# Neighbourhood scores of a hybrid attention block: a low part on 64 rows, or on both halves of 128

## The chip, the core and the metric

The kernel runs on one core of a Trainium2 chip. The metric is the device time of one execution in microseconds (us); less is better. Three runs are shown and their median is taken. The profile is of one execution more. Engine names are those of the profile: PE is TensorE's matmul side, PEld its weight loads, DVE is VectorE, ACT is ScalarE, POOL is GpSimd, and SP issues the DMAs.

## What is computed

Two layers of a block for 256 image tokens (a 4 x 64 grid) and 256 context tokens, 1024 wide, in float32. In each layer both streams are normed and modulated, projected, sent through three branches (neighbourhood attention, a gated MLP, a low-rank attention called MLA), merged by gates, projected out, and sent through a squared-ReLU MLP. In the second layer only the image stream is finished. The part that matters here is the neighbourhood attention with 8 heads of 64 dims:

```python
q_na = rms_norm(split_heads(cols(p, OFF_NA_Q, NA_WIDTH), NA_HEADS), na_q_gain[i])
k_na = rms_norm(split_heads(cols(p, OFF_NA_K, NA_WIDTH), NA_HEADS), na_k_gain[i])
...
s_loc = jnp.einsum('bhqd,bhkcd->bhqkc', q_r, k_band).astype(jnp.float32) * scale + bias
s_loc = jnp.where(col_in[:, None, :], s_loc, NEG_INF).reshape(b, h, GRID_W, kh * GRID_W)
s_ctx = jnp.einsum('bhqd,bhld->bhql', q_r, k_ctx).astype(jnp.float32) * scale
p = jax.nn.softmax(jnp.concatenate([s_loc, s_ctx], axis=-1), axis=-1).astype(v.dtype)
```

In the first layer the context's queries attend to the context's keys too, without the bias.

## The kernel before

**Products in two parts.** Most products take float32 operands as a sum of two float32r tiles, a high part H and a low part L (`split1`, L115 and L116: ACT writes `wh`, DVE subtracts to get `wl`). A product of two such operands is three matmuls: H by H, H by L, L by H (`mm3`, L276 to L278). These carry nearly all of PE's time: the projections (`b_ps`, `u`), the gates and branch products (`gate`, `z`), the output (`o_ps`) and the MLP (`f`).

**Scores.** Heads have 64 dims, and the array has 128 rows, so the score product is packed. `na_keys` (L352) puts a head's H part on the head's own half of the partitions (rows 0 to 63 for even heads, 64 to 127 for odd ones) and its L part on the other half, in one tile `naK`. `na_queries` (L367) transposes two heads at a time into PSUM (`tr_ps`), lets ACT write the query's H part on both halves of a tile `naQ` (L377, L378), and lets DVE write the L part on the head's own half of a tile `naQL` that two heads share (L379). `na_score` (L384) then needs two matmuls for a score block: `naQ` by `naK` over 128 rows (L389: H by H and H by L in one), and `naQL` by `naK` over the 64 rows of the head's half (L390: L by H). Both add into the same PSUM tile `S`.

**Attention.** `soft_pv` (L406) works on two heads at a time. For each stream (image, then in the first layer context) and each of two query tiles it makes one score block per head, 512 keys wide for the image and 256 for the context. DVE adds the bias (L422, image only) and takes the negated maximum (L424), ACT takes the exponential (L427), DVE the reciprocal and the scaling (L429, L430), PE transposes (`pt`, L433), ACT copies to `PT` (L435), and PE multiplies by the values (`pv`, L439). PSUM has two buffers for `S`, one for `pt` and one for `pv`. So there are 4 x 2 x 2 x 2 = 32 score blocks in the first layer, 16 of them 512 wide and 16 of them 256 wide, and 16 blocks of 512 in the second: 48 in all.

**Order.** Each engine runs its instructions in one fixed order, which a scheduler wrote when the program was built. It lays the gate and branch products of the first four `merge` chunks (L442) between the steps of the attention, so that PE has work while DVE and ACT run the softmax. The query tiles are made earlier, between the projections: near 97 to 115 us in the first layer and 968 to 977 us in the second. `bg` puts blocks of the modulation product between them (`mod_ps`, L137, each matmul on 32 of the array's columns).

**Buffers.** `naK`, `naQ` and `naQL` come from a pool of 34 tiles of 128 x 512 (`g2`). The pool with the tag "ymix" has 8 tiles of 128 x 512: `merge` keeps its 8 sums there (L457), and in between the next layer's modulation uses them.

Of the kernel before, what the change touches and what calls it, by code (L numbers as in the profile page):

```python
# [15 lines left out]
NT = 512  # L16
# [10 lines left out]
def hybrid_block_kernel(tc, a, out):  # L27
# [6 lines left out]
    with ExitStack() as es:  # L34
# [19 lines left out]
        def views(name, T):  # L54
            """room for tiles [128, T], two in a tile where they fit."""
            while True:
                t = g2(name)
                if T == NX:
                    yield t[:, 0:NX]
                    yield t[:, NX:]  # L60
                else:
                    yield t

        def parts(name, T):
            """room for the H and L parts of [128, T]."""
            v = views(name, T)
            return next(v), next(v)
# [3 lines left out]

        # constants
        ident = cp.tile([128, 128], F32, name="ident")
# [5 lines left out]

        # stationary silu(c), silu(c_ctx)  # L80
        cin = cp.tile([128, KC, 2], F32, name="cin")
# [26 lines left out]
        def split(raw, width=512):  # L108
            """the two halves of a block as exact H + L parts."""
            return [split1(raw[:, i * width:(i + 1) * width], width) for i in range(2)]  # L110
# [7 lines left out]

        # background work: the modulation vectors, one weight block at a time
        background = []  # L120
# [19 lines left out]
        def mod_finish(ps, w, dsts, modT, bmod, streams):  # L140
            """dsts: per 128 columns i, slices of chunks for j = 0..3."""
            t = tmp2("mod_sb")
            vec.tensor_copy(t[:, :w], ps[:, :w])
            pst = psum("s", "mod_t")
            for i in range(w // 128):
                nc.tensor.transpose(pst[:, i * 128:(i + 1) * 128], t[:, i * 128:(i + 1) * 128], ident)
            for i in range(w // 128):
                v4 = pst[:, i * 128:(i + 1) * 128].rearrange("p (j r) -> p j r", j=4)
                for v in range(streams):
                    o, b = dsts(modT[:, v, :], i), dsts(bmod, i)  # L150
                    i0 = v4[:, :, v]
                    if len(o.shape) == 3:
                        i0 = i0.rearrange("p (a b) -> p a b", a=2)
                    vec.tensor_tensor(out=o, in0=i0, in1=b, op=ALU.add)

        def mod_quarter(l, q, modT, bmod, streams):
            """shift and scale of norm1, dims 256 q .. 256 q + 255."""
            ps = psum("pt", "mod_ps")
            for kb in range(4):
                for kk in range(2):  # L160
                    raw = g2("rawm", F32)
                    nc.sync.dma_start(out=raw, in_=a["wmod1"][l, q, kb][:, kk * 512:kk * 512 + 512])
                    mod_cols(ps, raw, 0, 128, 2 * kb + kk)
                yield
            mod_finish(ps, 128, lambda m, i: m[:, 0:16].rearrange("p (a c) -> p a c", a=2)[:, :, 2 * q:2 * q + 2], modT,
                       bmod, streams)
# [10 lines left out]
        def mod_pooled(l, g, modT, bmod, streams):  # L177
            """column block g (0, 1: half of shift and scale of norm1 each; else a vector of its own)."""
            accs = [[xp.tile([128, NT], F32, tag="ymix", name="macc", bufs=8) for _ in range(2)] for _ in range(streams)]
# [41 lines left out]
        def norm_stream(acc, v, pb):  # L221
            """acc: per-dim sums of squares; gives rsqrt(mean + eps) of the stream's tokens on every partition."""
            ps = psum("s", "st_ps")
# [34 lines left out]
        def h_chunk(h, c, v, pb, gain, modT, sh0):  # L258
            """H/L parts of a chunk of modulate(rms_norm(x))."""
            s = slice(v * NX, (v + 1) * NX)  # L260
# [29 lines left out]
        def paced(marks, n, free=0):  # L290
            """steps of which the first ones are free and n are spread over the marked instructions."""
            return iter([None] * free + [marks[i * len(marks) // n] for i in range(n)])

        def gemm_b(blocks, hH, hL, tts, width, widths=None, mid=None, pre=None):
            """tokens on the partitions; blocks of two k chunks [128, 2 * width]."""
            pss = {t: psum("mm", "b_ps") for t in tts}
# [18 lines left out]
        def rstd_heads(ss, n):  # L315
            """ss [128, n] already mean + eps."""
            rs = sp.tile([128, 32], F32, tag="rsh", name="rsh")
# [3 lines left out]
        def na_heads(pss, name):  # L321
            """per-head rms norm of [tokens, 512] and its transpose, in pairs of heads."""
            tts = list(pss)
# [19 lines left out]
        def transposed(tiles, c0, w):  # L343
            """columns c0 .. c0 + w of the token tiles, with the tokens on the free axis."""
            ps = psum("s", "tr_ps")
# [6 lines left out]
        def na_keys(tiles, gain):  # L352
            """per head the H and L parts stacked on the contraction, H on the head's own half."""
            res = []
# [12 lines left out]
        def na_queries(tiles, gain):  # L367
            """per head the H part on both halves of the contraction, and the L parts of a pair."""
            res = []
            W = 128 * len(tiles)  # L370
            room, roomL = views("naQ", W), views("naQL", W)
            for j in range(4):
                ps = transposed(list(tiles.values()), j * 128, 128)
                QL = next(roomL)
                for p, q in ((lo, hi), (hi, lo)):
                    Q = next(room)
                    act(out=Q[p, :W], in_=ps[p, :W], func=AF.Copy, scale=gain[p])  # L377
                    act(out=Q[q, :W], in_=ps[p, :W], func=AF.Copy, scale=gain[p])  # L378
                    vec.scalar_tensor_tensor(out=QL[p, :W], in0=ps[p, :W], scalar=gain[p], in1=Q[p, :W], op0=ALU.mult,  # L379
                                             op1=ALU.subtract)  # L380
                    res.append((Q, QL))
            return res

        def na_score(K, Q, h):  # L384
            p = (lo, hi)[h % 2]
            (Qs, QL), Ks = Q[h], K[h]

            def score(s, q0, k0, nk):
                mm(s, lhsT=Qs[:, q0:q0 + 128], rhs=Ks[:, k0:k0 + nk], start=True, stop=False)  # L389
                return mm(s, lhsT=QL[p, q0:q0 + 128], rhs=Ks[p, k0:k0 + nk], start=False, stop=True)  # L390

# [14 lines left out]
        def soft_pv(score, V, pv, streams, bias, marks):  # L406
            """one pair of heads; pv gets the transposed outputs."""
            for v in range(streams):
# [100 lines left out]
        for l in range(L):  # L509
# [5 lines left out]
            hH, hL = h1  # L515
            # NA keys, queries, values
            def wb(m):
# [25 lines left out]

            # per-layer constants: additive term of the spatial gating: ln_b * rowsum(w_s) + b_s
            rsum = psum("s", "rsum")
# [4 lines left out]

            # gain columns, with the attention scales in the queries' ones
            sc_na = 0.125
# [38 lines left out]

            # MLA down-projections
            cps = gemm_b([a["wc"][l, i] for i in range(4)], hH, hL, [0, 1, 2, 3], 416,
# [21 lines left out]
            def swapped_products(dst, src, w, t, nh):  # L615
                """dst = swap(src) * rS for a tail [128, nh, 32]."""
                for hf in range(2):
# [31 lines left out]

            # gated MLP  # L650
            ckv, cq = [], []
# [46 lines left out]

            # neighbourhood attention
            ynH, ynL = [], []  # L700
# [18 lines left out]

            # MLA keys and values  # L720
            ukv = split(load(a["ukv"][l]))
# [76 lines left out]

            # MLA attention
            ymH, ymL = [], []  # L800
# [12 lines left out]

            # output projection, residual, statistics of the next norm
            bg_all()
# [15 lines left out]
            def out_chunk(block, n, xh, xl, vs, mod0, stats):  # L831
                """one chunk of 128 output dims for the streams vs, added to the residual."""
                ws = split(load(block))
# [11 lines left out]
            if last:  # L845
                # the norm's factor per token comes after the product here: relu(rstd * (w1 . gx) + w1 . shift),
                # the shift riding along as one more token
                aa2 = gains(col[:, 16:24], modT, 32, 0)
# [22 lines left out]

            # ffn
            if not last:
# [69 lines left out]
def _layout(i):  # L943
# [37 lines left out]
    r["ukv"] = A(f["mla_w_ukv"])  # L981
    # local bias: the gathered table inside the window, the masked value outside
    q = np.arange(NX)
# [42 lines left out]
```

## Time and profile before

| | |
|---|---|
| runs (us) | 1436.35, 1433.31, 1435.72 |
| median (us) | 1435.72 |
| span of the profiled execution (us) | 1433.4 |
| PE busy (us) | 1406.2 |
| DVE busy (us) | 950.1 |
| ACT busy (us) | 705.3 |
| granted TensorE clock over the span | 1.000 |

The span reaches from the first to the last instruction of the program in the profiled execution. No time of its own is kept for that execution beside its span, so what lies around the span can't be read; the median of the runs stands 2.3 us above it, and the runs themselves are 3.0 us apart. PE's matmuls are pipelined and their ends are modelled: how long one costs is read from its start to the next one's start, not from its duration.

### The profile page before, as it was taken

The numbers are of one execution on the slowest core, as the hardware profiler recorded it, in microseconds if no ns is written. First come the engines' busy times: TensorE is split into PE (matmuls) and PEld (weight loads), VectorE is DVE, ScalarE is ACT, GpSimd is POOL, SyncE is SP. The second block draws the span as 40 slices with busy tenths as digits, with TensorE's granted clock in tenths as the row PEclk, the third lists the DMA queues.
The fourth block names the chain that finished last, engine by engine and source line by source line (L and its number), as shares of the span: only waits on it lengthen the run. The fifth ranks groups of instructions, "written<-read, shape, count | busy, mean of one in ns | idle before, by whom it ended". The sixth has DMA issues, their size and how long they took to land.

```text
span 1433.4 us, 22556 instructions
## 1 busy us (share of the span) xinstructions
PE 1406.2 (98%) x8438; PEld 1166.7 (81%) x8438; DVE 950.1 (66%) x2059; ACT 705.3 (49%) x1440; POOL 58.4 (4%) x35
## 2 busy tenths in 40 slices
PE   6999999999999999999999999999999999999999
PEld 4888755777667779987788888988868879999998
DVE  5655465665553548897766665686777766777765
ACT  4466254543443336633324234566666655656654
POOL 0110000110000000000000000011002100000000
PEclk9999999999999999999999999999999999999999
DMA  9423532133312455665555553442532424666654
GB/s 334 141 73 108 206 118 75 61 108 122 114 45 89 143 180 158 197 200 169 203 177 204 180 202 90 147 149 89 180 104 81 135 87 140 194 180 178 187 182 147
DMA packets 67213, 210.61 MB, mean 147 GB/s; under 512 B 8609, under 2 KB 9633, under 8 KB 67105
## 3 DMA queue, kind: packets, MB, share of 16 engines
q1 hardware_dynamic: 67104, 209.18, 45.6%
q8 instruction: 66, 1.08, 0.3%
q14 instruction: 43, 0.34, 0.1%
HBM read 208.10 MB, written 1.05 MB: 146 GB/s over the span
## 4 chain that ended last, share of the span: by engine, by line
PE 91%; DMA 4%; DVE 3%; issue 1%; ACT 1%; SPq 1%; POOL 0%; DVEq 0%; ACTq 0%
PE o_ps L277 7%; PE o_ps L278 7%; PE o_ps L276 7%; PE gate L276 5%; PE f L276 5%; PE f L277 5%; PE f L278 5%; PE gate L277 5%; PE gate L278 5%; PE b_ps L276 4%; PE b_ps L277 4%; PE b_ps L278 4%; DMA rawx<-in_wmod_dram 3%; PE pt L433 3%; PE z L276 3%; PE S L396 3%
## 5 line engine op out<-in xcount | busy, mean ns | idle before, releaser
L115 ACT ACTIVATE wh<-raw 128x512 fp32r<-128x512 f32 (+2 forms) x570 | 352.8, 626 | 520.9 <-PE o_ps L277 185.4
L116 DVE TENSOR_TENSOR wl<-raw,wh 128x512 fp32r<-128x512 f32 (+2 forms) x570 | 385.4, 683 | 181.7 <-ACT wh L115 162.9
L276 PE MATMUL f<-hH,wh 128*128 128x258 f32 (+2 forms) x560 | 180.7, 324 | 0.5 <-ACT wh L115 0.5
L278 PE MATMUL f<-hH,wl 128*128 128x258 f32 (+2 forms) x560 | 180.8, 323 | 0.1
L277 PE MATMUL f<-hL,wh 128*128 128x258 f32 (+2 forms) x560 | 180.6, 324 | 0.2 <-DVE hL L266 0.2
L277 PE MATMUL o_ps<-aL,wh 128*128 128x256 f32 (+1 forms) x544 | 176.3, 327 | 1.9 <-DVE aL L895 1.9
L276 PE MATMUL o_ps<-aH,wh 128*128 128x256 f32 (+1 forms) x544 | 175.8, 328 | 0.0
L278 PE MATMUL o_ps<-aH,wl 128*128 128x256 f32 (+1 forms) x544 | 175.5, 327 | 0.0
L276 PE MATMUL gate<-hH,wh 128*128 128x512 f32 (+1 forms) x384 | 143.2, 373 | 0.1
L277 PE MATMUL gate<-hL,wh 128*128 128x512 f32 (+1 forms) x384 | 130.4, 339 | 0.0
L278 PE MATMUL gate<-hH,wl 128*128 128x512 f32 (+1 forms) x384 | 130.3, 339 | 0.0
L276 PEld LDWEIGHTS f<-hH,wh 128*128 128x128 f32 x560 | 105.9, 190 | 10.1 <-ACT wh L115 2.0
L277 PEld LDWEIGHTS f<-hL,wh 128*128 128x128 f32 x560 | 105.9, 190 | 8.8 <-DVE hL L266 0.4
L278 PEld LDWEIGHTS f<-hH,wl 128*128 128x128 f32 x560 | 106.1, 190 | 8.5 <-DVE wl L116 0.3
L277 PEld LDWEIGHTS o_ps<-aL,wh 128*128 128x128 f32 x544 | 103.0, 190 | 11.0 <-DVE aL L895 2.3
L276 PEld LDWEIGHTS o_ps<-aH,wh 128*128 128x128 f32 x544 | 102.4, 190 | 10.0 <-ACT wh L115 1.2
L278 PEld LDWEIGHTS o_ps<-aH,wl 128*128 128x128 f32 x544 | 102.7, 190 | 8.8
L277 PE MATMUL b_ps<-wl,hH 128*128 128x512 f32 (+2 forms) x288 | 108.5, 380 | 0.0
L197 DVE SCALAR_TENSOR_TENSOR macc<-rawx,sS,macc 128x512 f32<-128x512 f32 x112 | 78.9, 748 | 41.1 <-DMA rawx<-in_wmod_dram 41.1
L278 PE MATMUL b_ps<-wh,hL 128*128 128x512 f32 (+2 forms) x288 | 106.1, 380 | 0.0
L276 PE MATMUL b_ps<-wh,hH 128*128 128x512 f32 (+2 forms) x288 | 102.8, 385 | 0.0
L435 ACT ACTIVATE PT<-pt 128x512 f32<-128x512 f32 (+1 forms) x96 | 50.5, 526 | 87.8 <-PE pt L433 87.3
(226 smaller groups left out, 2525.2 us busy)
## 6 DMA issues: line engine op xcount, KB each, us to landing
raw<-in_wa_dram SPq DMA_DIRECT2D x147, 512.0 KB, 3.6
raw<-in_w_dram SPq DMA_DIRECT2D x68, 512.0 KB, 3.6
raw<-in_wb_dram SPq DMA_DIRECT2D x32, 512.0 KB, 3.3
raw<-in_wmod_dram SPq DMA_DIRECT2D x32, 512.0 KB, 3.2
rawx<-in_wmod_dram SPq DMA_DIRECT2D x32, 512.0 KB, 4.7
raw<-in_wo_dram SPq DMA_DIRECT2D x24, 512.0 KB, 3.6
rawm<-in_wmod_dram SPq DMA_DIRECT2D x32, 256.0 KB, 6.0
rawx<-in_wmod_dram SPq DMA_DIRECT2D x32, 256.0 KB, 4.2
```

The lines of the kernel that those rows point to most:

```text
L115: act(out=wh[:, :width], in_=src, func=AF.Copy)
L116: vec.tensor_tensor(out=wl[:, :width], in0=src, in1=wh[:, :width], op=ALU.subtract)
L197: vec.scalar_tensor_tensor(out=o, in0=src, scalar=s, in1=o, op0=ALU.mult, op1=ALU.add)
L276: mm(ps, lhsT=sh, rhs=mh, start=first, stop=False)
L277: mm(ps, lhsT=sh, rhs=ml, start=False, stop=False)
L278: mm(ps, lhsT=sl, rhs=mh, start=False, stop=last)
L396: return mm(s, lhsT=Q[h][0:96, q0:q0 + 128], rhs=K[h][0:96, k0:k0 + nk], start=True, stop=True)
L433: nc.tensor.transpose(pt[:, i * 128:(i + 1) * 128], P[:, i * 128:(i + 1) * 128], ident)
L435: act(out=PT[hh][:, :n, qt * 128:(qt + 1) * 128], in_=pt[:, :nk].rearrange("p (i q) -> p i q", i=n), func=AF.Copy)
```

## The change

The query's L part of a head now stands on both halves of a tile, so that its product with `naK` runs over all 128 rows. `naK` holds the key's L part on the other half, so that the second matmul now adds L by L as well. Each head has a `naQL` tile of its own. DVE writes it in two subtractions instead of one (the second reads the same PSUM rows and writes the other half of the partitions). The first four heads' tiles come from the pool of 34 as before; those of the last four come from the "ymix" pool: four tiles in the first layer, two halves in each of two tiles in the second. Comments and docstrings were removed as well; a line of the changed kernel behind this function has a number 10 higher.

```diff
+            def spare(name):
+                t = xp.tile([128, NT], F32R, tag="ymix", name=name, bufs=8)
+                return [t[:, 0:NX], t[:, NX:]] if W == NX else [t]
+
             room, roomL = views("naQ", W), views("naQL", W)
+            late = []
             for j in range(4):
                 ps = transposed(list(tiles.values()), j * 128, 128)
-                QL = next(roomL)
                 for p, q in ((lo, hi), (hi, lo)):
                     Q = next(room)
+                    if len(res) < 4:
+                        QL = next(roomL)
+                    else:
+                        late = late or spare("naQL2")
+                        QL = late.pop(0)
                     act(out=Q[p, :W], in_=ps[p, :W], func=AF.Copy, scale=gain[p])
                     act(out=Q[q, :W], in_=ps[p, :W], func=AF.Copy, scale=gain[p])
-                    vec.scalar_tensor_tensor(out=QL[p, :W], in0=ps[p, :W], scalar=gain[p], in1=Q[p, :W], op0=ALU.mult,
-                                             op1=ALU.subtract)
+                    for o in (p, q):
+                        vec.scalar_tensor_tensor(out=QL[o, :W], in0=ps[p, :W], scalar=gain[p], in1=Q[p, :W],
+                                                 op0=ALU.mult, op1=ALU.subtract)
                     res.append((Q, QL))
             return res
 
         def na_score(K, Q, h):
-            p = (lo, hi)[h % 2]
             (Qs, QL), Ks = Q[h], K[h]
 
             def score(s, q0, k0, nk):
                 mm(s, lhsT=Qs[:, q0:q0 + 128], rhs=Ks[:, k0:k0 + nk], start=True, stop=False)
-                return mm(s, lhsT=QL[p, q0:q0 + 128], rhs=Ks[p, k0:k0 + nk], start=False, stop=True)
+                return mm(s, lhsT=QL[:, q0:q0 + 128], rhs=Ks[:, k0:k0 + nk], start=False, stop=True)
```

On DVE, where the first layer's query tiles are made (`wl` is a weight block's low part, for the projections that run meanwhile), the rows before were these:

```order
L116 TENSOR_TENSOR wl<-raw,wh 128x416 x2
L379 SCALAR_TENSOR_TENSOR naQL<-tr_ps,gq,naQ 64x512
L116 TENSOR_TENSOR wl<-raw,wh 128x416
L379 SCALAR_TENSOR_TENSOR naQL<-tr_ps,gq,naQ 64x512 x2
L116 TENSOR_TENSOR wl<-raw,wh 128x416
L379 SCALAR_TENSOR_TENSOR naQL<-tr_ps,gq,naQ 64x512 x2
L116 TENSOR_TENSOR wl<-raw,wh 128x416 x2
```

The same place now:

```order
L116 TENSOR_TENSOR wl<-raw,wh 128x416 x2
L390 SCALAR_TENSOR_TENSOR naQL<-tr_ps,gq,naQ 64x512 x2
L116 TENSOR_TENSOR wl<-raw,wh 128x416 x2
L390 SCALAR_TENSOR_TENSOR naQL<-tr_ps,gq,naQ 64x512 x4
L116 TENSOR_TENSOR wl<-raw,wh 128x416 x2
L390 SCALAR_TENSOR_TENSOR naQL<-tr_ps,gq,naQ 64x512 x2
L390 SCALAR_TENSOR_TENSOR naQL_1064<-tr_ps,gq,naQ 64x512 x2
L116 TENSOR_TENSOR wl<-raw,wh 128x416 x2
```

Each subtraction stands there twice, and up to four of them now stand together ahead of two `wl`, where at most two stood together.

On PE, early in the first layer's attention, a run of rows before (`gate` is a gate product of `merge`, `pt` a transpose of the softmax, `mod_ps` the modulation):

```order
L390 MATMUL S<-naK,naQL 128x512
L276 MATMUL gate<-hH,wh 128x512
L277 MATMUL gate<-hL,wh 128x512
L278 MATMUL gate<-hH,wl 128x512
L433 MATMUL pt<-ident,P 128x128 x4
L137 MATMUL mod_ps<-raw,sS 32x256 x4
L433 MATMUL pt<-ident,P 128x128 x4
L389 MATMUL S<-naK,naQ 128x256
L390 MATMUL S<-naK,naQL 128x256
```

And now (the size in a row is that of the output, which doesn't tell the rows of the array that are used):

```order
L400 MATMUL S<-naK,naQL 128x512
L276 MATMUL gate<-hH,wh 128x512
L277 MATMUL gate<-hL,wh 128x512
L278 MATMUL gate<-hH,wl 128x512
L443 MATMUL pt<-ident,P 128x128 x4
L137 MATMUL mod_ps<-raw,sS 32x256 x4
L443 MATMUL pt<-ident,P 128x128 x4
L399 MATMUL S<-naK,naQ 128x256
L400 MATMUL S<-naK,naQL 128x256
```

Nothing moved there, and nothing moved anywhere in the two attentions, on any engine. Away from the places where query tiles are made (on PE and ACT some steps of the first layer's projections changed places with the query transposes there), every engine's order is what it was; POOL's and SP's have no difference at all.

## Rows read from the trace of the kernel before

**Rows 1.** The page's first part: busy us, share of the span, instructions.

```profile
PE 1406.2 (98%) x8438; PEld 1166.7 (81%) x8438; DVE 950.1 (66%) x2059; ACT 705.3 (49%) x1440; POOL 58.4 (4%) x35
```

**Rows 2.** The first attention as one window: busy us by engine, clock, DMA.

```profile
180.00:262.00 82.00, 81.30 (x397) 49.21 (x397) 50.94 (x129) 43.94 (x111) 0.00 (x0) 1.00 0.29 90
```

**Rows 3.** Groups by form: the 64-row score product (busy us, mean ns | idle).

```profile
L390 PE MATMUL S<-naK,naQL 64*128 64x512 f32 x32 | 15.9, 496 | 0.0
...
L390 PE MATMUL S<-naK,naQL 64*128 64x256 f32 x16 | 6.1, 380 | 0.0
```

**Rows 4.** Timeline of PE around a 512-wide score block: start us, us, what.

```profile
188.31 0.39 PE L278 MATMUL gate<-hH,wl 128*128 128x512 f32 x1
188.54 0.40 PE L389 MATMUL S<-naK,naQ 128*128 128x512 f32 x1
188.87 0.50 PE L390 MATMUL S<-naK,naQL 64*128 64x512 f32 x1
189.30 0.50 PE L276 MATMUL gate<-hH,wh 128*128 128x512 f32 x1
189.63 0.40 PE L277 MATMUL gate<-hL,wh 128*128 128x512 f32 x1
```

**Rows 5.** Timeline of the weight loads at the same block.

```profile
188.87 0.18 PEld L390 LDWEIGHTS S<-naK,naQL 64*128 64x128 f32 x1 [0.36 <-issue]
```

**Rows 6.** Timeline of PE around a 256-wide score block's second product.

```profile
192.67 0.38 PE L390 MATMUL S<-naK,naQL 64*128 64x256 f32 x1
192.98 0.50 PE L276 MATMUL gate<-hH,wh 128*128 128x512 f32 x1
193.32 0.40 PE L277 MATMUL gate<-hL,wh 128*128 128x512 f32 x1
```

**Rows 7.** Timeline of PE in an even stream of 256-wide products.

```profile
1023.11 0.28 PE L276 MATMUL u<-hH,wh 128*128 128x256 f32 x1
1023.23 0.28 PE L277 MATMUL u<-hL,wh 128*128 128x256 f32 x1
```

**Rows 8.** Timeline of PE where products on 32 columns follow a full one.

```profile
186.00 0.39 PE L278 MATMUL gate<-hH,wl 128*128 128x512 f32 x1
186.32 0.64 PE L137 MATMUL mod_ps<-raw,sS 128*32 128x256 f32 x8
```

**Rows 9.** Groups of DVE by form: the query's low part.

```profile
L379 DVE SCALAR_TENSOR_TENSOR naQL<-tr_ps,gq,naQ 64x512 fp32r<-64x512 f32 x8 | 6.0, 749 | 9.5 <-ACT naQ L378 9.5
L379 DVE SCALAR_TENSOR_TENSOR naQL<-tr_ps,gq,naQ 64x256 fp32r<-64x256 f32 x8 | 3.9, 484 | 4.6 <-ACT naQ L378 4.5
```

**Rows 10.** Timeline of DVE and PE while the first layer's query tiles are made.

```profile
108.29 1.07 DVE L116 TENSOR_TENSOR wl<-raw,wh 128x416 fp32r<-128x416 f32 x2
...
110.05 0.76 DVE L379 SCALAR_TENSOR_TENSOR naQL<-tr_ps,gq,naQ 64x512 fp32r<-64x512 f32 x1 [0.68 <-ACT naQ L378]
...
111.17 0.35 PE L277 MATMUL b_ps<-wl,hH 128*128 128x416 f32 x1
```

**Rows 11.** Timeline of PE and ACT in a dense part of the first attention.

```profile
200.90 0.36 PE L389 MATMUL S<-naK,naQ 128*128 128x256 f32 x1
...
202.27 0.63 ACT L115 ACTIVATE wh<-raw 128x512 fp32r<-128x512 f32 x1 [0.19 <-PE gate L277]
...
202.44 0.48 PE L389 MATMUL S<-naK,naQ 128*128 128x512 f32 x1
...
203.55 0.48 ACT L427 ACTIVATE P<-S,nm 128x256 f32<-128x256 f32 x1
...
204.22 0.48 PE L389 MATMUL S<-naK,naQ 128*128 128x512 f32 x1
```

**Rows 12.** Timeline of PE: the only wait over 0.15 us in the first attention.

```profile
191.40 0.64 PE L137 MATMUL mod_ps<-raw,sS 128*32 128x256 f32 x8 [0.70 <-DMA raw<-in_wmod_dram]
```

**Rows 13.** Timeline of DVE and PE at the second attention's first wait.

```profile
1037.01 0.43 DVE L422 TENSOR_TENSOR S<-S,bias 128x256 f32<-128x256 f32 x1 [0.35 <-PE S L390]
...
1040.39 0.49 PE L389 MATMUL S<-naK,naQ 128*128 128x512 f32 x1 [1.13 <-ACT P L427]
```

## Prediction, made before the changed kernel ran

> **What bounds the kernel now.** I read the page's first part first. PE is busy for 1406.2 of 1433.4 us [rows 1], so a change counts if it shortens what PE does, or if it makes PE wait. The first attention as a window of its own says the same: PE 81.3 of 82.0 us, DVE 50.9, ACT 43.9, granted clock 1.00, which is the 2.4 GHz level, DMA share 0.29 [rows 2]. DVE and ACT have room there on average. But a busy PE is not a PE at its peak, since the ends of matmuls are modelled. So I then read the timeline of PE and took the distance from one start to the next.
>
> In a run of full products 512 wide the starts are 0.23 us apart: 188.31, 188.54 [rows 4]. At the score block this breaks. The first score product, on 128 rows, takes until 188.87, 0.33. The second, on 64 rows, takes until 189.30, 0.43, though it streams the same 512 columns. The gate product behind it takes until 189.63, 0.33, though it is a full one like its neighbours. The third view is that of the weight loads: the one for the 64-row product begins at 188.87, together with its matmul and not under the product before it, and PEld was idle for 0.36 ahead of it with no one to wait for [rows 5]. So a product on 64 rows between products on 128 doesn't overlap with them: the one ahead runs out, the load lies open, and the next load lies open again. The 64 rows themselves are not cheap either: 496 ns mean against the 0.40 of its neighbours [rows 3, 4].
>
> **What the change takes away.** The three products take 1.09 (188.54 to 189.63) where three in a stream take 0.69. If the second one has the same shape as its neighbours, that is 0.40 less: 0.10 ahead of it, 0.20 in it, 0.10 behind it. For the 256-wide blocks I read the last two: 0.31 from 192.67 to 192.98 and 0.34 from there to 193.32 [rows 6], where a 256-wide product in a stream takes 0.12 [rows 7] and a 512-wide one 0.23. That is 0.19 and 0.11, the same sum, so the price doesn't hang on the width and I use 0.40 for both. There are 32 and 16 such products [rows 3], 48 x 0.40 = 19.2 us. Where a block has transposes or 32-column products beside it, a delay of theirs stays, but the change of shape within the block goes all the same. The lower bound of the price is that only the two open loads go: 0.30, or 14.4 in all.
>
> That it is the change of shape, and not something in the low part's tile, is shown by other products: a full gate product followed by one on 32 columns takes 0.32, from 186.00 to 186.32, where it takes 0.23 otherwise [rows 8]. That is the same 0.09 to 0.10 as ahead of the 64-row product.
>
> A rule of the Trainium skill bears on the new product. "TensorE: Matmul & The Clock Gate", Part 3, The mechanism, says that a weight load overlaps with a running matmul only when the two stand on different row groups. By that rule a 128-row load would lie open behind a 128-row product; what it would do here is a rival below. The stream in [rows 4] disagrees with it, since full products follow each other there at 0.23 us.
>
> **What the change adds.** DVE makes 8 subtractions of 64x512 and 8 of 64x256 more, 6.0 and 3.9 us by the groups of the ones that are there [rows 9]: 9.9 us. The second one writes another half of the partitions than it reads; that form isn't among these rows, and I take the same duration. What covers it is the DVE's own idle time: it waits for ACT's `naQ` ahead of each (9.5 and 4.6 us in sum, in the same rows). What is queued behind is `wl`, and PE waits for that. PE's nearest use in the first layer is at 111.17, of the first of two tiles that DVE made in 1.07 from 108.29 on, so that it was done by 108.9: 2.3 us of room [rows 10]. In the new order up to four subtractions stand ahead of two `wl` where two stood, 1.5 us more, less an idle time like the 0.68 there. That is under 2.3, so I cost it at nothing. With the cover gone it would be 9.9. The query tiles themselves are first read tens of us later in either layer, so that their lateness costs nothing. ACT does as many instructions as before, DMAs and queues are untouched.
>
> **What the change uncovers.** PE comes 0.40 earlier per block, and the softmax must follow. I looked in the timeline for the places where a score block finds its PSUM buffer only just free. In the dense part of the first attention PE starts a block at 204.22; the exponential that freed its buffer began at 203.55 and took 0.48, so it had ended 0.19 before [rows 11]. Between 200.90 and 204.22 PE does two blocks and would come 0.80 earlier. ACT has only 0.19 of idle time to close in that stretch, ahead of 202.27, and that one waits for PE. So 0.80 - 0.19 - 0.19 = 0.42 turns into a wait. The same pattern stands three more times in that attention: 4 x 0.42 = 1.7 us.
>
> A modulation block's DMA is already late by 0.70 at 191.40 [rows 12]. It is issued when the modulation products begun at 186.32 have let go of their buffer [rows 8], and two blocks lie between, so that this wait grows by 0.80.
>
> In the second attention PE waits at 1040.39 for an exponential [rows 13]. Two blocks lie ahead of it, 0.80. The chain behind the exponential goes through DVE, which idled 0.35 for the second block at 1037.01, so it can come at most 0.35 earlier, and 0.45 is lost. The attention's other wait of this kind hangs on a gate product behind both blocks and moves with PE.
>
> Together 1.7 + 0.8 + 0.45 = 3.0 us are given back. **The sum:** -19.2 + 3.0 = -16.2 us. On the profiled execution that is 1433.4 to 1417.2; on the median of the runs, 2.3 us above that span, 1435.7 to 1419.5.
>
> **The rivals.**
>
> *Nothing is given back.* ACT and DVE could make up more than I count, since both have idle time around the dense parts. Against it: the orders are fixed, and the idle time lies elsewhere. It gives 1435.7 - 19.2 = 1416.5.
>
> *The softmax becomes the bound.* If in each two blocks the second one's gain turns into a wait, as in the dense part, 24 x 0.40 = 9.6 is lost, and the DMA's 0.8: 1435.7 - 19.2 + 10.4 = 1426.9. For it: DVE and ACT work in the same order as before, and the room of 0.19 is already small. Against: outside the four dense parts each has idle time to give, as the averages in [rows 2] say.
>
> *The second product's load lies open all the same.* Then its 0.20 stays and each block gives the 0.20 around it: 48 x 0.20 = 9.6, 1426.1, with less to give back. Against it: the full load of the product at 188.54 didn't make that one late behind another full product [rows 4]. It is what the rule from Part 3 would make of this kernel.
>
> *The change doesn't do what it says.* If the open load belonged to the low part's tile or to the second product of a pair, all would stay: 1435.7. Against it: [rows 8], and the product behind, which has nothing to do with that tile and is late as well.
>
> *Halves that would have run together.* Two products on opposite halves of the rows could run side by side, and the full ones can't. Then the 64-row products cost half of their stream time now and the whole later: 32 x 0.23 + 16 x 0.12 = 9.3, half of it 4.6 lost, and nothing gained: 1440.3. It decides if two of them stand next to each other. In the order they never do: a full product follows each, and in [rows 4] each takes longer than a full one. "TensorEngine Tiling (Array Packing)", Overview, of the Trainium skill promises up to twice the speed for a contraction of 64 or less, which speaks against giving the tiling up. By that rule the time would be the 1440.3; the trace shows no overlap to lose.
>
> *Slower, by the buffers.* The four tiles `naQL2` of the first layer sit in the pool of `merge`'s sums until the last score. If one of the first four chunks needed such a buffer, DVE would block at L457, and three chunks of 36 products would come behind the attention instead of between its steps: 3 x 36 x 0.23 = 24.8, so 1435.7 + 24.8 - 19.2 = 1441.3. It decides whether four tiles and four chunks fit in the 8 buffers. They do, just, and the order of the instructions shows no such wait.
>
> **How the numbers follow.** My forecast 0.58; nothing given back 0.15; softmax the bound 0.13; the open load 0.03; no effect 0.05; halves 0.02; buffers 0.04. The predicted time is the forecast's, 1419.5. The range goes from 1416.5 to 1426.9, widened by half the spread of the runs (1.5) at the top and twice that at the bottom, for prices read to 0.01 us: 1413.5 to 1428.4. It leaves out the last three. About 0.2%, 2.9 us, is what a measurement of this kernel can tell from no change. Faster by more than that: 0.58 + 0.15 + 0.13 + 0.03 = 0.89; within it 0.05; slower 0.06.
>
> **What would show it.** In the profile after: the second score product is on 128*128, its start 0.23 behind the first in a stream, its weight load under the product before; the first attention's window ends some 10 us earlier and the second's some 6; PE's waits for `P` L427 appear in the first attention with 1 to 3 us. DVE's group L390 counts 32, with no PE wait for `wl` between 97 and 125 us. I am wrong if the product behind a score block still takes 0.33, if PE waits for more than 6 us in the two attentions, or if PE waits for `wl` where the query tiles are made.

## The result and the profile after

The changed kernel takes 1419.24 us (median of 4 runs, 1417.8 to 1419.85) against 1435.22 us of the kernel before beside it (4 runs, 1433.31 to 1436.35). The ratio is 0.9878, with a 95% interval of 0.9855 to 0.9902: 16.0 us faster, where 16.2 were forecast. The profiled execution has a span of 1417.8 us and took 1419.85 us, so that 2.05 us lie around the span.

The page's first part after, to be laid beside [rows 1]:

```profile
PE 1391.1 (98%) x8438; PEld 1165.7 (82%) x8438; DVE 958.9 (68%) x2075; ACT 703.1 (50%) x1440; POOL 58.4 (4%) x35
```

PE has the same 8438 instructions and 15.1 us less to do. DVE has 16 more and 8.8 us more. The two attentions as windows, from the first score product to the start of the last (window, its length, then busy us of PE, PEld, DVE, ACT and POOL with their instructions, the granted clock, DMA share, GB/s). Before:

```profile
180.90:263.00 82.10, 81.40 (x400) 48.96 (x398) 50.80 (x129) 43.29 (x109) 0.00 (x0) 1.00 0.29 90
1034.90:1080.00 45.10, 42.55 (x250) 29.56 (x249) 32.57 (x78) 26.13 (x59) 0.00 (x0) 1.00 0.34 104
```

After:

```profile
181.60:254.00 72.40, 70.91 (x400) 46.89 (x398) 50.56 (x130) 43.31 (x110) 0.00 (x0) 1.00 0.31 102
1025.00:1064.70 39.70, 37.20 (x250) 29.68 (x248) 31.73 (x78) 25.59 (x59) 0.00 (x0) 1.00 0.37 118
```

The first one has shrunk from 82.1 to 72.4 and the second from 45.1 to 39.7, with nearly the same work on DVE and ACT in them. (The window of [rows 2] begins 0.9 ahead of the first score product and ends 1.0 ahead of the last.) Around the same score block as in [rows 4], PE's timeline is now this:

```profile
188.24 0.39 PE L278 MATMUL gate<-hH,wl 128*128 128x512 f32 x1
188.47 0.39 PE L399 MATMUL S<-naK,naQ 128*128 128x512 f32 x1
188.70 0.39 PE L400 MATMUL S<-naK,naQL 128*128 128x512 f32 x1
188.93 0.39 PE L276 MATMUL gate<-hH,wh 128*128 128x512 f32 x1
189.15 0.39 PE L277 MATMUL gate<-hL,wh 128*128 128x512 f32 x1
```

The starts are 0.23, 0.23, 0.23 and 0.22 apart; the 0.33, 0.43 and 0.33 are gone. The weight load of the second product, beside [rows 5]:

```profile
188.48 0.19 PEld L400 LDWEIGHTS S<-naK,naQL 128*128 128x128 f32 x1
```

It begins at 188.48, under the product that began at 188.47, and no idle time stands before it. A full load of 128 rows is thus hidden behind a product on the same 128 rows. The rule of the Trainium skill that the prediction weighed ("TensorE: Matmul & The Clock Gate", Part 3, The mechanism: overlap only on different row groups) would have it open; this row disagrees.

A 256-wide block, beside [rows 6]:

```profile
192.58 0.28 PE L400 MATMUL S<-naK,naQL 128*128 128x256 f32 x1
192.70 0.40 PE L276 MATMUL gate<-hH,wh 128*128 128x512 f32 x1
192.93 0.40 PE L277 MATMUL gate<-hL,wh 128*128 128x512 f32 x1
```

0.31 and 0.34 have become 0.12 and 0.23. Laid start against start with the trace of before, the 48 blocks gain 0.381 us each on average, 18.3 in all.

**What was given back.** The waits view of PE for the first attention lists only one wait over 0.3 us, the one of [rows 12], now longer:

```profile
191.40 0.64 PE L137 MATMUL mod_ps<-raw,sS 128*32 128x256 f32 x8 [1.19 <-DMA raw<-in_wmod_dram]
```

32 x 0.381 = 12.2 were gained there, though, and the attention ended only 10.0 earlier. The rest doesn't stand in the waits view, because the modelled ends of PE's matmuls cover it. It shows when each instruction's start is laid against its start before. In nine places PE falls back by 0.07 to 0.32 us, 1.5 us together, beside 0.5 at the wait above. Three of them, on the timeline of all engines:

```profile
193.16 0.68 ACT L437 ACTIVATE P<-S,nm 128x512 f32<-128x512 f32 x1
...
193.98 0.39 PE L399 MATMUL S<-naK,naQ 128*128 128x256 f32 x1
...
202.34 0.49 ACT L437 ACTIVATE P<-S,nm 128x256 f32<-128x256 f32 x1
...
202.98 0.50 PE L399 MATMUL S<-naK,naQ 128*128 128x512 f32 x1
...
210.87 0.48 DVE L440 TENSOR_SCALAR P<-P,r 128x512 f32<-128x512 f32 x1
...
211.50 0.52 PE L443 MATMUL pt<-ident,P 128*128 128x128 f32 x3
```

The score product at 202.98 answers to the one at 204.22 in [rows 11]. Each of the three begins 0.14 or 0.15 after the end of the exponential or of the scaling above it (193.84, 202.83, 211.35): PE now stands at the softmax's heels, and these three cost 0.23, 0.32 and 0.24. In the second attention, PE's timeline, the first row beside [rows 13]:

```profile
1029.97 0.50 PE L399 MATMUL S<-naK,naQ 128*128 128x512 f32 x1 [1.13 <-ACT P L437]
...
1034.92 0.50 PE L399 MATMUL S<-naK,naQ 128*128 128x512 f32 x1 [0.73 <-ACT P L437]
```

The first of the two waits is as long as before, although two blocks ahead of it became 0.77 shorter; the start came only 0.45 earlier against the attention's first product. The timeline of DVE and PE shows where the rest went:

```profile
1026.26 0.76 DVE L432 TENSOR_TENSOR S<-S,bias 128x256 f32<-128x256 f32 x2
...
1026.93 0.42 DVE L705 TENSOR_TENSOR yg<-yg 128x256 fp32r<-128x256 f32 x1
...
1027.40 0.39 PE L277 MATMUL z<-yg,wh 128*128 128x256 f32 x1
```

The idle time of 0.35 that DVE had ahead of the second bias addition ([rows 13]) is gone. PE's branch product stands 0.05 behind the end of DVE's `yg` and has lost 0.31 there, 2.6 us ahead of the wait. The attention gained 16 x 0.383 = 6.1, and the first product behind its last block (`kv`, at 1066.97) came 5.5 earlier; 0.20 of the difference is lost at that product, which also waits.

**Three things that aren't the change's.** The start of the program was 0.71 later in this execution, in its DMAs. In the execution of before, PE waited for DVE's `aL` ahead of an output product:

```profile
715.07 0.50 PE L277 MATMUL o_ps<-aL,wh 128*128 128x512 f32 x1 [1.88 <-DVE aL L895]
```

This execution has no such wait there; that product and the one behind it come 2.15 us earlier against their surroundings. And the granted clock fell once. Windows of the changed kernel around that place:

```profile
290.00:295.60 5.60, 3.59 (x24) 3.02 (x23) 5.29 (x18) 4.06 (x10) 0.62 (x1) 0.99 0.39 108
295.60:299.00 3.40, 3.40 (x10) 2.72 (x9) 3.40 (x9) 3.02 (x7) 0.51 (x1) 0.52 0.32 130
299.00:305.00 6.00, 6.00 (x28) 4.92 (x28) 4.24 (x7) 1.75 (x3) 3.04 (x2) 1.00 0.27 87
```

and PE's timeline there:

```profile
293.60 0.64 PE L765 MATMUL h_tr<-ident,knat 128*96 128x128 f32 x4 [1.75 <-DVE kml L769]
...
295.79 0.63 PE L276 MATMUL gate<-hH,wh 128*128 128x512 f32 x1
296.21 0.63 PE L277 MATMUL gate<-hL,wh 128*128 128x512 f32 x1
```

For 3.4 us the clock is at its 1.2 GHz level, and 512-wide products come every 0.42 instead of 0.23. PE had waited 1.75 us shortly ahead. This stretch costs some 1.6 us by the offsets of the starts. The three together are +0.71 - 2.15 + 1.6 = +0.2.

### The profile page after: what moved, and what is told of

Same layout as the page of the kernel before. It is cut to its first block, busy times and chain, and to the rows that moved or that the text cites. A ratio compares the mean times of both kernels' runs of the same rounds, so it can differ in the third digit from the quotient of the medians.

```text
span 1417.8 us, 22572 instructions
## 1 busy us (share of the span) xinstructions
PE 1391.1 (98%) x8438; PEld 1165.7 (82%) x8438; DVE 958.9 (68%) x2075; ACT 703.1 (50%) x1440; POOL 58.4 (4%) x35
## 4 chain that ended last, share of the span: by engine, by line
PE 96%; DVE 2%; DMA 1%; ACT 1%; issue 0%; SPq 0%; POOL 0%; DVEq 0%; ACTq 0%
PE o_ps L276 8%; PE o_ps L278 8%; PE o_ps L277 8%; PE f L276 6%; PE f L277 6%; PE f L278 6%; PE gate L276 5%; PE gate L277 5%; PE gate L278 5%; PE b_ps L276 4%; PE b_ps L277 4%; PE b_ps L278 4%; PE pt L443 3%; PE S L406 3%; PE z L276 2%; PE z L277 2%
## 5 line engine op out<-in xcount | busy, mean ns | idle before, releaser
L276 PEld LDWEIGHTS f<-hH,wh 128*128 128x128 f32 x560 | 105.9, 189 | 10.2 <-ACT wh L115 2.0
L276 PEld LDWEIGHTS o_ps<-aH,wh 128*128 128x128 f32 x544 | 102.4, 190 | 10.2 <-ACT wh L115 1.2
```

The costliest lines, as they stand in the source:

```text
L276: mm(ps, lhsT=sh, rhs=mh, start=first, stop=False)
```

## The experiments

Lengths below are from the start of an attention's first score product to the start of its last one's first matmul, in the one profiled execution of each kernel; before, they are 82.05 and 45.04 us, after 72.37 and 39.71.

**The change once more**, beside the kernels of the next three parts on one chip.

> The changed kernel again, for comparison on the same chip. 1419 us. If the stretch at half the granted clock near 296 us in its first profile belongs to the kernel, it is there again; if it is chance, it is gone and the span is 1.6 us shorter than the time of the run would otherwise say.

1420.19 us (1419.99 to 1420.4), ratio 0.9889 with 0.9874 to 0.9904. Lengths 72.54 and 39.71; no stretch at a lower clock in its profile. The span isn't 1.6 us shorter for that (1418.4): the wait for `aL` is there again, with 1.57 us. The wait for the modulation block's DMA was 1.56 here, 0.37 more than in the first profile of the same kernel.

**Only the tiles.** The new tiles, buffers and subtractions stay, the product goes back to 64 rows:

```diff
+            p = (lo, hi)[h % 2]
-                return mm(s, lhsT=QL[:, q0:q0 + 128], rhs=Ks[:, k0:k0 + nk], start=False, stop=True)
+                return mm(s, lhsT=QL[p, q0:q0 + 128], rhs=Ks[p, k0:k0 + nk], start=False, stop=True)
```

> The query tiles as changed (a low part on both halves, 16 more subtractions, four tiles from the other pool), the second score product on 64 rows as before. If the change of the array's shape is what cost, nothing is gained: 1435 us, within 2, and the products around a score block take 0.33, 0.43, 0.33 us as before. If the tiles, the buffers or the order of the instructions made the gain, it comes here too: 1419. If the 16 subtractions lie open, it is slower than before by up to 9.9: 1445.

1436.22 us (1432.1 to 1439.01), ratio 1.0003 with 0.9991 to 1.0015; lengths 81.78 and 45.04. Its PE timeline has the old pattern back:

```profile
187.29 0.40 PE L400 MATMUL S<-naK,naQ 128*128 128x512 f32 x1
187.62 0.50 PE L401 MATMUL S<-naK,naQL 64*128 64x512 f32 x1
188.05 0.50 PE L276 MATMUL gate<-hH,wh 128*128 128x512 f32 x1
188.38 0.40 PE L277 MATMUL gate<-hL,wh 128*128 128x512 f32 x1
```

0.33, 0.43, 0.33, with the low part on both halves of its tile. So neither the tile nor its place makes the old product slow, and the 16 subtractions, the "ymix" buffers and the few steps that changed places are worth nothing measurable on their own.

**Only the first layer.** `na_queries` and `na_score` take the new form in the first layer and the old one in the second:

```diff
-                    for o in (p, q):
+                    for o in (p, q) if both else (p,):
...
+            p = slice(0, 128) if both else (lo, hi)[h % 2]
...
-                qT.extend(na_queries(qnat, gq[:, 0:1]))
+                qT.extend(na_queries(qnat, gq[:, 0:1], l == 0))
```

> The change in the first layer alone. If each block gives its own 0.38 us, 32 of 48 blocks give 12.2, less some 2.2 that the softmax and a DMA give back: 10 us faster than before, 1425, with the second attention as before. If the gain came from elsewhere (a wait that happened to go in the later MLP), it doesn't follow the blocks: near 1419 or near 1435.

1429.09 us (1425.21 to 1430.06), ratio 0.9947 with 0.9932 to 0.9962: 4 us above what was expected. The first attention is as in the changed kernel, 71.86. The second is 46.55, 1.5 longer than before. Its profile holds two stretches of 3.4 us at the 1.2 GHz level, at 706 us and this one in the second attention (windows, columns as above):

```profile
1033.80:1037.20 3.40, 3.40 (x15) 3.06 (x14) 2.82 (x7) 1.11 (x3) 0.00 (x0) 0.50 0.30 77
```

If each costs 1.6 us like the one above, they are 3.2 of the 4 us missed. The one run of the six whose mean clock was highest, 0.999, took 1425.21, the time expected. So the shares of the two attentions do add up, as far as this tells; the median itself doesn't show it, and why this kernel meets such stretches in most runs stays open.

**Only the product.** The kernel before, with the second product over all 128 rows of the tile that two heads share, and no subtraction more:

```diff
-            p = (lo, hi)[h % 2]
...
-                return mm(s, lhsT=QL[p, q0:q0 + 128], rhs=Ks[p, k0:k0 + nk], start=False, stop=True)
+                return mm(s, lhsT=QL[:, q0:q0 + 128], rhs=Ks[:, k0:k0 + nk], start=False, stop=True)
```

> The second score product on 128 rows, but with the tile of before that two heads share, and no more subtractions than before. Each head's score then also takes in the other head's query low part times its own key's low part. If the shape is the cause and the subtractions are hidden, the time is that of the changed kernel: 1419, within 1.5. If the subtractions cost anything, it is faster than the changed kernel, by 9.9 at the most: 1409. If a tile per head is what matters, it is as before: 1435.

1420.23 us (1419.93 to 1420.65), ratio 0.989 with 0.9875 to 0.9905, against 1420.19 of the change on the same chip. Its groups by form:

```profile
L389 PE MATMUL S<-naK,naQL 128*128 128x512 f32 x32 | 12.8, 399 | 0.0
...
L379 DVE SCALAR_TENSOR_TENSOR naQL<-tr_ps,gq,naQ 64x512 fp32r<-64x512 f32 x8 | 6.0, 750 | 9.5 <-ACT naQ L378 9.5
```

DVE is as in [rows 9], the product as in the changed kernel. The whole gain is in the shape of the product, and DVE's 9.9 us more are free. Lengths 71.46 and 41.28, the second with 3.4 us at the lower clock from 1029.0 in it. Run again with the last two kernels below, the same kernel had 71.69 and 39.70:

> The kernel with the second score product on 128 rows from the shared tile again, for comparison on the same chip: 1420.2, within 1.

1419.79 us (1416.39 to 1424.54), ratio 0.989 with 0.9871 to 0.9908.

**Two halves next to each other.** The rival that halves could run together, put to the test: the first products of both heads of a pair come first, then the two 64-row products, one behind the other:

```diff
-                    S = []
-                    for hh in range(2):
-                        s = psum("s", "S")
-                        marks.append(score[hh](s[:, :nk], q0, k0, nk).ins)
-                        S.append(s)
+                    S = [psum("s", "S") for hh in range(2)]
+                    low = [score[hh](S[hh][:, :nk], q0, k0, nk) for hh in range(2)]
+                    with tc.issue_after(high[-1].ins) if bias is not None else nullcontext():
+                        ends = [f() for f in low]
```

> The kernel before, with the neighbourhood scores in another order: the first products of two heads, then the two second products on 64 rows, one on the lower and one on the upper half, side by side. A head's softmax now starts only after both. If the cost is a change of shape, it is paid once for two blocks: some 0.2 us ahead of and behind the pair, and 0.2 to 0.4 less per pair than 0.76; on PE alone 24 x 0.3 = 7 us less than before. If halves of the rows run together, the pair takes one stream of 0.23 and not two: 24 x 0.2 = 5 us less again. The softmax that starts later gives part of it back, which the trace tells apart.

And the same order with full products on the shared tile:

> The same order of instructions as the last kernel on every engine, with the second products on 128 rows (from the tile that two heads share, so that the other head's query low part times the own key's low part comes in too). If only the change of shape costs, the two products take 0.23 each between full products, and this kernel is faster than the last one. If two halves run together at no more than one stream, the last one is as fast or faster than this one by up to 5 us.

With halves 1438.6 us (1436.98 to 1441.61), ratio 1.0018 with 1.0005 to 1.0031; with full products 1434.89 (1432.11 to 1436.19), ratio 0.9991 with 0.9977 to 1.0005. So the order with halves is slower than before, where PE alone was expected to gain 7 or more, and the one with full products can't be told from before, though the same products in the old order gain 16. The new order costs about that much: the first head's softmax starts later, and in the first attention of the kernel with full products PE waits 3.1 us for ACT ahead of transposes and 2.2 ahead of scores. What makes up the rest of its cost wasn't traced. The two differ only in the rows, and PE's timelines show what that is worth. Halves:

```profile
223.03 0.50 PE L391 MATMUL S<-naK,naQ 128*128 128x512 f32 x1
223.46 0.50 PE L392 MATMUL S<-naK,naQL 64*128 64x512 f32 x2
223.89 0.50 PE L276 MATMUL gate<-hH,wh 128*128 128x512 f32 x1
224.22 0.40 PE L277 MATMUL gate<-hL,wh 128*128 128x512 f32 x1
```

Full products:

```profile
223.09 0.50 PE L391 MATMUL S<-naK,naQ 128*128 128x512 f32 x1
223.43 0.62 PE L392 MATMUL S<-naK,naQL 128*128 128x512 f32 x2
223.89 0.40 PE L276 MATMUL gate<-hH,wh 128*128 128x512 f32 x1
224.12 0.39 PE L277 MATMUL gate<-hL,wh 128*128 128x512 f32 x1
```

The two halves do run together: they start 0.003 us apart and take 0.43 as a pair with their open load, where two full ones take 0.46. But the change of shape is paid ahead (0.43 against 0.34) and behind (0.33 against 0.23). From the first row to the last it is 1.19 against 1.03: 0.16 lost in this pair. By the starts of all instructions the eight 256-wide pairs lose 0.28 to 0.30 each and the sixteen 512-wide ones 0.14 to 0.17, but for one with 32-column products behind it, which loses nothing, and one at the lower clock. The medians are 3.7 apart, the same way; the sums can't be compared more closely, since ahead of the program's end the profile of the kernel with halves holds 10.2 us at the lower clock and the other none. "TensorEngine Tiling (Array Packing)", Key Properties, of the Trainium skill says that tiles work in parallel and that a change of the tiling drains TensorE. Both agree with these rows; the price, some 0.2 us around a pair and 0.2 for its load, is theirs.

**The late modulation block.** Only the product, and a fourth buffer for the `raw` tiles (the pool of 34 gives up two):

```diff
-            return gp.tile([128, 512], dt, tag="g", name=name, bufs=34)
+            return gp.tile([128, 512], dt, tag="g", name=name, bufs=32)
...
-                raw = wp.tile([128, 1024], F32, tag="raw", name="raw", bufs=3)
+                raw = wp.tile([128, 1024], F32, tag="raw", name="raw", bufs=4)
```

> The kernel with the second score product on 128 rows from the shared tile, with four buffers for raw weight blocks instead of three (and 32 tiles instead of 34 in the other pool). If the modulation block that came late in the first attention waits for a buffer, that wait of 1.2 us goes, and with it some of the later ones: 1 to 4 us faster than with three buffers, 1415 to 1418. If loads are late for another reason, or the pool of 32 makes new waits, 1419 or more.

1419.66 us (1418.18 to 1422.37), ratio 0.9886 with 0.9866 to 0.9907. Nothing that can be measured: the one wait became two of 0.45, and the first attention took 72.49.

**ACT relieved.** If ACT sets the small waits, copies of `PT` moved to DVE should shorten them. Only the product, with the second head's copies on DVE in both attentions:

```diff
-                        act(out=PT[hh][:, :n, qt * 128:(qt + 1) * 128],
-                            in_=pt[:, :nk].rearrange("p (i q) -> p i q", i=n), func=AF.Copy)
+                        o, i0 = PT[hh][:, :n, qt * 128:(qt + 1) * 128], pt[:, :nk].rearrange("p (i q) -> p i q", i=n)
+                        if bias is not None and hh:
+                            vec.tensor_copy(o, i0)
+                        else:
+                            act(out=o, in_=i0, func=AF.Copy)
```

> The kernel with the second score product on 128 rows from the shared tile, with the copies of one of two heads' transposed weights moved from ACT to DVE in the neighbourhood attentions (24 of them). If ACT's work in the dense parts is what gives back some 2 us of the gain, part of that comes out as time: 1 to 2 us faster than with all copies on ACT, 1418 to 1419, and PE waits less for P. If DVE has no room there, its own work comes later and it is slower: 1422 or more.

1440.5 us (1436.39 to 1443.13), ratio 1.003 with 1.0017 to 1.0042; lengths 82.32 and 45.15. The timeline of PE and ACT shows why:

```profile
202.32 0.44 PE L432 MATMUL pt<-ident,P 128*128 128x128 f32 x2
...
202.85 0.38 ACT L438 ACTIVATE PT<-pt 128x256 f32<-128x256 f32 x1 [1.42 <-PE pt L432]
...
203.29 0.44 PE L432 MATMUL pt<-ident,P 128*128 128x128 f32 x2 [0.54 <-ACT PT L438]
```

The scheduler laid the two heads' transposes next to each other, and there is one `pt` buffer. PE waits 13.5 us in 20 such places. So this kernel tells what that order costs, and nothing of ACT. The second try leaves the pair alone and moves the copies of the context stream (`if bias is not None and v`), in the first layer:

> The same, with only the context stream's copies moved to DVE (16 of 256 columns, first layer alone), since DVE adds no bias there and the dense parts are there. If ACT is the limit in them, the first attention is shorter by 0.5 to 1.7 us and the second the same: 1418.5 to 1419.7. If not, 1420.2 as with all copies on ACT.

1420.39 us (1418.97 to 1426.16), ratio 0.9895 with 0.9879 to 0.9912. The first attention is 74.41, 2.7 longer than 71.69 of the kernel without the copies beside it: PE waits 0.9 for the exponential in one place that had no wait, 0.4 more for the modulation block, and twice 0.69 for the `pt` buffer, where two heads' transposes follow each other as above. So this kernel, too, tells mostly what an order costs. The time of the whole shows no difference. By what the changed kernel's timeline shows, two of the small waits are behind DVE's scaling, so that more work on DVE is no way out; how much of the rest is ACT's own isn't settled by either.

## Why the prediction was right, step by step

**What bounds the kernel: right.** 18.3 us less between PE's starts made the whole some 15.6 shorter.

**48 x 0.40 = 19.2: the mechanism right, the size 0.9 too large.** The change of shape was the cause: only the tiles gives 1.0003, only the product 0.989. Measured were 0.381 a block, 18.3. The blocks read for the price had full products on both sides; where a transpose or a 32-column product stands beside the block, less than 0.10 goes on that side, as the prediction allowed for but didn't count.

**DVE's 9.9 at nothing: right.** The change and the product alone are 0.04 us apart. The groups of DVE by form in the changed kernel, beside [rows 9]:

```profile
L390 DVE SCALAR_TENSOR_TENSOR naQL<-tr_ps,gq,naQ 64x512 fp32r<-64x512 f32 x16 | 12.0, 750 | 7.0 <-ACT naQ L388 6.7
L390 DVE SCALAR_TENSOR_TENSOR naQL<-tr_ps,gq,naQ 64x256 fp32r<-64x256 f32 x16 | 7.7, 483 | 2.3 <-ACT naQ L388 2.0
```

The subtraction that writes the other half takes the same 750 and 483 ns, and the idle time ahead shrank from 9.5 and 4.6 to 7.0 and 2.3. Where the tiles are made, beside [rows 10]:

```profile
103.91 3.06 DVE L390 SCALAR_TENSOR_TENSOR naQL<-tr_ps,gq,naQ 64x512 fp32r<-64x512 f32 x4 [0.81 <-ACT naQ L388]
107.00 1.09 DVE L116 TENSOR_TENSOR wl<-raw,wh 128x416 fp32r<-128x416 f32 x2
```

Four subtractions stand ahead of two `wl`, and PE has no wait for `wl` there.

**The dense parts, 4 x 0.42 = 1.7: the sum near, the places not.** The one that was read lost 0.39 (0.07 and 0.32, at the second and third score block of [rows 11]). Three other score products behind transposes lost 0.07 each. The rest stands at four other places with 0.19 to 0.24 each, two behind an exponential and two behind DVE's scaling, which the prediction didn't name. Together 1.5. "Waits for `P` with 1 to 3 us in the first attention" failed as it was put: the waits view shows none of them, and they are read only from start to start.

**The DMA, 0.8: the trigger right, the size 0.5 here.** The load of the late block is issued as the prediction said. SyncE's timeline, before and after:

```profile
187.02 0.33 SPq L103 DMA_DIRECT2D raw<-in_wmod_dram  x1
```

```profile
187.15 0.33 SPq L103 DMA_DIRECT2D raw<-in_wmod_dram  x1
```

Both stand 0.70 behind the start of the modulation products ahead of them (186.32 and 186.45), and so do those of the changed kernel's second execution and of the kernels with only the tiles, only the first layer and only the product. From there PE was ready for the next block 4.38 behind those products before (191.40 - 0.70 - 186.32) and 3.76 after, 0.62 earlier. The block's products could start 4.38 behind the issue before and 4.25 after, so that 0.13 of the 0.62 didn't become a wait, which grew by 0.49. That time from the issue on is what varies: in the four other executions with full products it was 3.34 to 4.44, and the wait 0.47 to 1.56. The wait of a single execution so says little about the term. Taken out of the lengths, the first attention is 71.0 to 71.2 in those five and 81.35 before, so that everything else in it repeats to 0.2.

**The second attention, 0.45: 0.6.** The chain through DVE was right: 0.31 was lost to it, ahead of the wait that was named and not at it. 0.20 stand at the product behind the last block, which the prediction didn't count, the rest in steps below 0.05. The attention's other wait moved with PE, as said.

**The sum.** 18.3 - 0.5 - 1.5 - 0.6 = 15.7, less the 0.2 of chance, 15.5; the spans are 15.6 apart. The forecast's 16.2 had two errors against each other: 0.9 too much gained, and 0.4 too much given back. That the first medians are 16.0 apart and meet the forecast to 0.2 us is luck beyond that: in the second measurement the changed kernel was 15.4 us faster.

**The rivals.** Nothing given back is refuted by the rows at 193.98, 202.98 and 211.50, though it is only 2.7 us away. Softmax the bound: 2.6 were given back, not 10.4. The open load is refuted by the load at 188.48, no effect and the buffers by the ratio and by only the tiles. Halves together: two halves side by side do run together, but in this kernel's order they never met, and where they do, a pair loses 0.16 or more against two full products.

## What to carry to other kernels

A product on half of the array's rows between full ones cost 0.38 us more than a full product here, on average over 48 places; filling the other half with a copy, or with something whose product is small enough to be added, was worth it, and an engine with idle time made the copy for nothing. Read the price of a matmul from its start to the next one's start, since neither its duration nor the waits view shows an open load or a drained pipe. What is gained on PE is partly handed to whatever follows closest behind it; the place that was read gave its term to 0.03, and the others had to be looked for in every instruction's start.

## What the runs showed of the hardware that was not expected

- With PE 98% busy, single stretches of 3.4 us (once 6.8) run at the 1.2 GHz level. The twelve profiles hold eight of them ahead of the program's last 2 us, and all eight stand at a wait of PE. Four begin 0.1 to 1.9 us behind the wait for DVE's `kml` that the first profile shows at 293.60 (1.75 us long; 2.21 in one): with the change, with halves side by side, with four `raw` buffers and with half of the copies on DVE. Three begin 0.6 to 0.7 behind the wait of 1.13 us in the second attention: with only the first layer, with only the product and with halves side by side (the one of 6.8). One begins at the end of a wait of 2.13 us for `aL`, with only the first layer. In the other profiles the same waits have no such stretch behind them, so that what decides it stays open. The one in the changed kernel costs some 1.6 us, a tenth of this change's gain.
- Two 64-row products on opposite halves start 0.003 us apart and take 0.43 us together with their load.
- A score product or transpose that waits for the exponential or for DVE's scaling starts 0.14 to 0.15 us after the end of what it waits for, at the places read here; the branch product behind DVE's `yg` starts 0.05 after. The 0.19 of room that the prediction read in [rows 11] was in truth nearly none.
